# A decoder trunk's mixing stage: every projection as three products of split operands

## The chip, the core and the metric

One core of one Trainium2 chip runs the whole program in one launch. The metric is the time of that launch in device microseconds (us); lower is better. Engines are named as in the profile: PE (matrix products), PEld (its weight loads), DVE (vector), ACT (scalar), POOL and SP; here nearly all transfers are issued by SP, whose queue is worked off in order.

## What is computed

Two layers of a decoder trunk on 256 tokens of 1024 channels, in float32. Of the reference, cut to one layer:

```
h = adaLN(rms_norm(x), c)                       # 256 x 1024
p = h @ w_in + b_in                             # 1792 RWKV, 512 q, 768 k/v, 24 gate, 2048 merge columns
ya = rwkv7_mix(p[rwkv]) @ w_up_rwkv             # 8 heads of 64, a recurrence over time
yb = nsa_mix(p[q], p[kv], p[gates]) @ w_up_nsa  # compressed, selected and window attention
x += gate * ((sigmoid(p[m0]) * ya + sigmoid(p[m1]) * yb) @ w_out)
x += gate2 * moe_ffn(adaLN2(rms_norm(x), c))    # 16 experts, top 2 of one group
```

The adaLN vectors are `c @ w_ada`, 48 columns of 128 per layer.

## The kernel before, in words

Activations lie transposed: channels on the partitions, the 256 tokens along the free axis, so a projection of 128 output columns is eight matmuls (one per 128 input channels, `NK` = 8). The normalized input is `hT`, 8 x 256 float32 per partition, made by `norm_apply`: per 128 channels one DVE instruction (L261) and one ACT instruction (L262).

The mixing stage of a layer has these parts, written as steps in the string `STEPS`:
- `x` (`channels`, by `proj`, L387) projects receptance, key and value of one pair of heads; `p` (`prep`) prepares a pair, `i` (`inverse`) solves its triangular systems in blocks, `c` (`chain`) runs its recurrence over four chunks of 64 tokens. There are four pairs of heads, 0 to 3.
- `k` (`compressed`) projects the keys and values for compression and the gates, `q` (`project`) the other keys, values and queries, both by `tok` (L709). Here the tokens are the stationary operand (128 of them) and the weights stream.
- `m` (`merges`) projects the 2048 merge columns, 16 products of 128 columns; `a` (`ada_step`) reduces one piece of `w_ada` on DVE (L224, four reductions of 1024 columns and an add).
- then attention: `KZ` (L913), scores (L957), softmax, `PTs` transposes, outputs into `ybT` (L996 to L1004).

There are two ways to make a float32 product. In `proj`, `tok` and the first six `merges` (L695) operands are float32. The last ten `merges`, and the up and out projections behind the mixing stage, use `split` (L266 on ACT, L267 on DVE): an operand is written as a rounded half `hi` of type fp32r and a remainder `lo`, and `mm3` (L279) adds three products, hi-hi, lo-hi and hi-lo. For that `hT` itself is split once, after the steps.

The order on each engine isn't the text's: the framework's scheduler interleaves the steps, by priority and its own estimate of when operands are there, and each engine then works off its list in order. Weights come in blocks of 1 MB: `ringa` (3 buffers) for `in_win` and `in_cmp`, `ringd` (1 buffer) for `in_ada`. A block is loaded again into a buffer only when its last reader is through. After the mixing stage come the up projections (y), the out projections, the router, and the experts, whose 96 MB per layer stream through 18 buffers.

## Time and profile before

| | |
|---|---|
| median of 3 runs | 1205.99 us (1205.66 to 1210.89) |
| the profiled execution, its own time | 1211.18 us |
| its span, first to last instruction | 1209.4 us |
| mean granted clock of PE, as a share of full speed | 0.964 |
| busy, share of the span | PE 92%, PEld 59%, DVE 51%, ACT 29%, POOL 7% |
| moved by DMA | 328.47 MB |

Read it by stage, not by the shares of the span: mixing, up and out projections, and experts have different limits. A busy PE is not PE at its peak, since matmuls are pipelined; so the spacing of matmuls in an unbroken run is what one costs. Each float32 matmul of the program stands as two rows in the trace (224 rows for 112 matmuls of `proj` in a layer), an fp32r matmul as one.

### The profile page before, as it was taken

Reading aid. Unit: us, or ns where it says so; the run is one execution under the profiler, and the core shown is the slowest. Engines: PE = TensorE matmul, PEld = TensorE weight load, DVE = VectorE, ACT = ScalarE, POOL = GpSimd, SP = SyncE. Lnnn points to the kernel's source line nnn. Section 1 sums busy time; section 2 is a strip of 40 time slices with the busy share of each in tenths; the row PEclk is TensorE's granted clock in tenths of the full one; section 3 lists DMA queues with packets and bytes.
Section 4 is the critical chain, followed back from the end, with each engine's and each line's share of the span. In section 5 each row is a group of like instructions: output and inputs, shape, how many; then the busy total and the mean of one; then the engine's idle time right before and its main releaser. Section 6 shows DMA issues by size and latency. Waiting matters only on the chain. (4 is left out here: it accounts for less than half of the span.)

```text
span 1209.4 us, 19271 instructions
## 1 busy us (share of the span) xinstructions
PE 1112.5 (92%) x7376; PEld 710.6 (59%) x7376; DVE 617.4 (51%) x1906; ACT 349.8 (29%) x878; POOL 88.3 (7%) x176
## 2 busy tenths in 40 slices
PE   6899999989896999999789999999999789999996
PEld 3776667777895343333257776777779743333432
DVE  0497788888665222121236777777658432212222
ACT  2423322257442120201024233213565411110110
POOL 0221220100000000000022201201000000000000
PEclk9999999999998999999969899899999989999998
DMA  9753564634784999999645346254246959999991
GB/s 389 278 174 140 219 235 175 244 139 175 313 347 180 419 420 420 419 420 420 261 164 208 141 182 236 105 201 183 70 180 263 393 205 420 419 420 419 420 409 39
DMA packets 47056, 328.47 MB, mean 272 GB/s; under 512 B 5216, under 2 KB 6880, under 8 KB 7904
## 3 DMA queue, kind: packets, MB, share of 16 engines
q1 hardware_dynamic: 46512, 326.83, 67.9%
q8 instruction: 62, 1.02, 0.3%
q14 instruction: 50, 0.41, 0.1%
q10 hardware_dynamic: 432, 0.21, 0.1%
HBM read 325.98 MB, written 1.05 MB: 270 GB/s over the span
## 5 line engine op out<-in xcount | busy, mean ns | idle before, releaser
L1324 PE MATMUL ps_mm<-w,xeA 128*64 128x512 f32 x512 | 127.1, 597 | 0.0
L1335 PE MATMUL ps_mm<-w,hb 128*64 128x512 f32 (+1 forms) x576 | 124.2, 604 | 1.5 <-DMA w<-in_exp 1.2
L387 PE MATMUL ps_mm<-hT,w 128*128 128x256 f32 x448 | 115.1, 402 | 3.8 <-ACT hT L262 3.8
L224 DVE CUSTOM_DVE_ANT_0 w<-w,crow 128x1024 f32<-128x1024 f32 x80 | 98.3, 1248 | 2.7 <-POOL crow L408 2.1
L1324 PE MATMUL ps_mm<-w,xeB 128*32 128x512 f32 (+1 forms) x640 | 97.8, 595 | 0.0
L387 PEld LDWEIGHTS ps_mm<-hT,w 128*128 128x128 f32 x448 | 84.7, 198 | 19.4 <-ACT hT L262 4.3
L709 PE MATMUL ps_mm<-w,hT 128*128 128x256 f32 x320 | 86.3, 401 | 0.0
L1335 PEld LDWEIGHTS ps_mm<-w,hb 128*64 128x64 f32 (+1 forms) x576 | 36.5, 126 | 74.6 <-issue 65.3
L267 DVE TENSOR_TENSOR ys<-ps_mm,ys 128x512 fp32r<-128x512 f32 x28 | 19.2, 686 | 111.3 <-ACT ys L266 111.3
L1324 PEld LDWEIGHTS ps_mm<-w,xeA 128*64 128x64 f32 x512 | 37.1, 136 | 65.1 <-issue 61.8
L267 DVE TENSOR_TENSOR w<-w,w 128x1024 fp32r<-128x1024 f32 (+1 forms) x68 | 65.5, 970 | 16.6 <-ACT w L266 16.6
L266 ACT ACTIVATE w<-w 128x1024 fp32r<-128x1024 f32 (+1 forms) x68 | 56.2, 852 | 39.2 <-PE ps_mm L279 39.2
L1278 DVE SCALAR_TENSOR_TENSOR hb<-hb,ps_mm 128x256 f32<-128x256 f32 x28 | 11.8, 421 | 103.5 <-ACT hb L1277 103.5
L709 PEld LDWEIGHTS ps_mm<-w,hT 128*128 128x128 f32 x320 | 57.0, 193 | 9.0 <-issue 1.5
L1300 DVE SCALAR_TENSOR_TENSOR xT<-ps_rw,gfh,xT 128x256 f32<-128x256 f32 x112 | 46.6, 477 | 25.2 <-PE ps_rw L1297 25.2
L1279 DVE SCALAR_TENSOR_TENSOR hb<-ps_mm,sw,hb 128x256 f32<-128x256 f32 x28 | 12.3, 479 | 86.5 <-PE ps_mm L1324 86.5
L1324 PEld LDWEIGHTS ps_mm<-w,xeB 128*32 128x32 f32 (+1 forms) x640 | 26.0, 115 | 51.8 <-issue 48.4
L266 ACT ACTIVATE ys<-ps_mm 128x512 fp32r<-128x512 f32 x28 | 16.7, 597 | 134.0 <-PE ps_mm L1335 110.0
L1297 PEld LDWEIGHTS ps_rw<-ohT,ys 128*128 128x128 f32 x224 | 31.4, 192 | 38.7 <-ACT ys L266 19.8
L279 PE MATMUL ps_mm<-h,w 128*128 128x256 f32 x336 | 49.2, 296 | 2.5 <-DVE w L267 1.4
L279 PE MATMUL ps_mm<-m,w 128*128 128x256 f32 x384 | 51.1, 287 | 0.0
L279 PE MATMUL ps_mm<-y,w 128*128 128x256 f32 x384 | 48.3, 288 | 2.8 <-ACT w L266 2.4
(407 smaller groups left out, 1865.5 us busy)
## 6 DMA issues: line engine op xcount, KB each, us to landing
w<-in_exp SPq DMA_DIRECT2D x192, 1024.0 KB, 19.7
w<-in_ada SPq DMA_DIRECT2D x48, 1024.0 KB, 5.0
w<-in_win SPq DMA_DIRECT2D x40, 1024.0 KB, 4.9
w<-in_cmp SPq DMA_DIRECT2D x8, 1024.0 KB, 5.6
w<-in_up SPq DMA_DIRECT2D x8, 1024.0 KB, 9.0
w<-in_out SPq DMA_DIRECT2D x8, 1024.0 KB, 5.8
row<-in_row SPq DMA_DIRECT2D x2, 780.0 KB, 7.4
mis<-in_mis SPq DMA_DIRECT2D x2, 752.0 KB, 6.8
```

What stands on the lines that cost most here:

```text
L224: ve.tensor_tensor_reduce(w[:, j, :], w[:, j, :], crow, 1.0, 0.0, op0=ALU.mult, op1=ALU.add, accum_out=mod[:, o:o + 1])
L266: ac.activation(hi, x, AF.Copy)
L267: e.tensor_sub(lo, x, hi.bitcast(F32))
L279: pe.matmul(out, lhsT=w2[i][:, k, :], rhs=x2[j][:, k, :], start=(k == ks[0] and not (i or j)), stop=(k == ks[-1] and j == 1), skip_group_c ...
L387: pe.matmul(p[:, 0:T], lhsT=w[:, k, o:o + 128], rhs=hT[:, k, 0:T], start=(k == 0), stop=(k == NK - 1))
L709: pe.matmul(p[:, po_:po_ + n], lhsT=hT[:, k, tt * 128:tt * 128 + 128], rhs=w[:, k, 0:n], start=(k == 0), stop=(k == NK - 1), skip_group_ch ...
L1278: ve.scalar_tensor_tensor(h[:, o], h[:, o], 1.0, p_g[:, o], op0=ALU.add, op1=ALU.mult)
L1279: ve.scalar_tensor_tensor(h[:, o], p_u[:, o], sw, h[:, o], op0=ALU.mult, op1=ALU.mult)
L1297: pe.matmul(p[:, i * 256:i * 256 + 256], lhsT=ys[:, n, o:o + 128], rhs=ohT, start=(n == 0), stop=(n == 1), skip_group_check=True)
L1300: ve.scalar_tensor_tensor(xT[:, d, :], p[:, i * 256:i * 256 + 256], gfh[:, d:d + 1], xT[:, d, :], op0=ALU.mult, op1=ALU.add)
L1324: pe.matmul(p[o:o + n, :], lhsT=xe[:, k, x:x + n], rhs=w[:, k % 4, :], start=(k == 0), stop=(k == NK - 1), skip_group_check=True)
L1335: pe.matmul(p2[n][o:o + m, :], lhsT=hsT[:, 2 * r + g, o:o + m], rhs=w[:, g, n * 512:n * 512 + 512], start=(r + g == 0), stop=(r + g == 2), ...
```

## The change

All projections of the mixing stage go through `split` and three products. `norm_apply` writes the two halves `h2` directly: DVE computes into a scratch tile, ACT adds the shift and rounds, DVE computes the remainder. `proj` and all 16 `merges` split each weight block of 8 x 128 columns first, into one of two pairs of buffers (`wsp`, open for the whole mixing stage). `project` takes 512 columns at a time (`in_win` blocks 8 to 11 are laid out 4 x 512 for it), in four parts of 1024 columns per partition, and both token halves, so it holds two PSUM banks; it runs twice instead of four times. `compressed` streams 256 columns and the 24 gate columns together, in three parts. `ybT` moves to another pool, `y2` no longer shares memory with `h2`; `m2`, `hth` and `htl` take the memory of `h2`. Four of the nine `a` steps leave the string.

```
-STEPS = "x0 p0 x1 p1 a i0 a i1 a k c0 a b x2 p2 h0 a i2 a c1 a x3 h1 p3 i3 a a q0 z c2 c3 q1 q2 q3 m6 r"
+STEPS = "x0 p0 x1 p1 a i0 a i1 k c0 a b x2 p2 h0 i2 a c1 x3 h1 p3 i3 a q0 z c2 c3 q1 m6 r"
...
-    def norm_apply(hT, pr, G, mod, sh0):
+    def norm_apply(h2, pr, G, mod, sh0):
...
-            h = hT[:, k, 0:T]
-            ve.scalar_tensor_tensor(h, xT[:, k, :], G[:, k:k + 1], pr[:, 0:T], op0=ALU.mult, op1=ALU.mult)
-            ac.activation(h, h, AF.Identity, bias=mod[:, sh0 + k:sh0 + k + 1])
+            t = tn.tile([128, T], F32, name="nt1", tag="nt1")
+            sh = mod[:, sh0 + k:sh0 + k + 1]
+            ve.scalar_tensor_tensor(t, xT[:, k, :], G[:, k:k + 1], pr[:, 0:T], op0=ALU.mult, op1=ALU.mult)
+            ac.activation(h2[0][:, k, :], t, AF.Identity, bias=sh)
+            ve.scalar_tensor_tensor(h2[1][:, k, :], t, sh, h2[0][:, k, :].bitcast(F32), op0=ALU.add, op1=ALU.subtract)
...
+        def parts(k, n):
+
+            return [wsp.tile([128, 1024], F32R, name=f"w2{i}", tag=f"w2{i}")[:, 0:k * n].rearrange("p (k n) -> p k n", k=k)
+                    for i in range(2)]
...
-            for k in range(NK):
-                pe.matmul(p[:, 0:T], lhsT=w[:, k, o:o + 128], rhs=hT[:, k, 0:T], start=(k == 0), stop=(k == NK - 1))
+            w2 = parts(NK, 128)
+            split(*w2, w[:, :, o:o + 128])
+            mm3(p[:, 0:T], w2, h2)
...
-        def tok(tt, w, n, p, po_):
-            for k in range(NK):
-                pe.matmul(p[:, po_:po_ + n], lhsT=hT[:, k, tt * 128:tt * 128 + 128], rhs=w[:, k, 0:n],
-                          start=(k == 0), stop=(k == NK - 1), skip_group_check=True)
+        def tok(p, w2, k0, kn, n):
+
+            for tt in range(2):
+                for k in range(k0, k0 + kn):
+                    for i, j in ((0, 0), (1, 0), (0, 1)):
+                        pe.matmul(p[tt][:, 0:n], lhsT=h2[j][:, k, tt * 128:tt * 128 + 128], rhs=w2[i][:, k - k0, :],
+                                  start=(k == 0 and not (i or j)), stop=(k == NK - 1 and j == 1), skip_group_check=True)
...
-            p = ps("mm")
+            p = [ps("mm") for _ in range(2)]
+            for k0 in range(0, NK, 2):
+                w2 = parts(2, 512)
+                split(*w2, wcol(8 + 2 * j + k0 // 4)[:, k0 % 4:k0 % 4 + 2])
+                tok(p, w2, k0, 2, 512)
...
-        for k in range(NK):
-            split(h2[0][:, k, :], h2[1][:, k, :], hT[:, k, 0:T])
```

How the instructions move, at three places. First DVE in layer 0, while the last pair of heads is in its inverse (`xt` and `X`: the steps of the 8 x 8 blocks; `rs_`: a reciprocal root; `UV`, `S`, `RB`: the recurrence; `w_`: halves of a weight block). Before:

```order
L579 TENSOR_TENSOR xt<-AB,X 128x4x5
L173 TENSOR_TENSOR rs_t<-rs_t,rs_h 32x1
L580 TENSOR_TENSOR X<-X,xt 128x4x5
L175 SCALAR_TENSOR_TENSOR rs_y<-rs_t,rs_i 32x1
L579 TENSOR_TENSOR xt<-AB,X 128x4x4
L172 TENSOR_TENSOR rs_t<-rs_y 32x1
L580 TENSOR_TENSOR X<-X,xt 128x4x4
```

And now:

```order
L591 TENSOR_TENSOR xt<-AB,X 128x4x6
L172 TENSOR_TENSOR rs_t<-rs_i 32x1
L270 TENSOR_TENSOR w_2564<-w,w_2563 128x1024
L592 TENSOR_TENSOR X<-X,xt 128x4x6
L173 TENSOR_TENSOR rs_t<-rs_t,rs_h 32x1
L650 TENSOR_TENSOR S<-S,ps_rc 128x64
L591 TENSOR_TENSOR xt<-AB,X 128x4x5
```

A weight split of 1024 columns stands between two steps that wait for each other, and the recurrence of another pair is mixed in.

Second DVE at the end of layer 0's attention, where the up projections follow (`y_`: halves of `yaT` and `ybT`; `lg`: a copy for the router; L224 as `ISA`: reductions of `w_ada`). Before:

```order
L224 ISA w,mod<-w,crow 128x1024
L224 ISA mod 128x1
L267 TENSOR_TENSOR w_2994<-w,w_2993 128x1024
L226 TENSOR_TENSOR mod<-mod,vec 128x4
L267 TENSOR_TENSOR w_3024<-w,w_3023 128x1024
L243 SCALAR_TENSOR_TENSOR ng<-mod,vec 128x8
L1089 COPY lg<-ps_rc 16x128
L267 TENSOR_TENSOR y_3072<-yaT,y_3071 128x256
```

And now:

```order
L226 TENSOR_TENSOR mod<-mod,vec 128x4
L270 TENSOR_TENSOR y_3563<-ybT,y_3562 128x256
L1094 COPY lg<-ps_rc 16x128
L270 TENSOR_TENSOR y_3563<-ybT,y_3562 128x256
L224 ISA w,mod<-w,crow 128x1024
L224 ISA mod 128x1
```

The last merge splits are gone from here and the splits of `yaT` stand earlier; four reductions of `w_ada` are left, two of them ahead of the first weight split of the up projections.

Third SP at the same place, the loads of `w_ada`, of the experts and of the up and out weights. Before:

```order
L159 DMA w<-in_ada 128x2048
L1054 DMA w<-in_exp 128x2048
L159 DMA w<-in_ada 128x2048 x2
L1054 DMA w<-in_exp 128x2048 x2
L159 DMA w<-in_up 128x2048 x4
```

And now:

```order
L1058 DMA w<-in_exp 128x2048
L159 DMA w<-in_ada 128x2048 x4
L159 DMA w<-in_up 128x2048 x2
L159 DMA w<-in_ada 128x2048
L159 DMA w<-in_up 128x2048 x2
```

One load of `w_ada` now stands between the loads of the up weights.

## Rows read from the trace of the kernel before

**Rows 1.** Windows by stage: of each engine busy us (x instructions), then clock, DMA share, GB/s.

```profile
core 0: us, PE busy (x) PEld busy (x) DVE busy (x) ACT busy (x) POOL busy (x), PEclk, DMA share, GB/s
34.00:60.00 26.00, 23.70 (x103) 19.72 (x104) 11.56 (x37) 12.88 (x31) 8.58 (x22) 0.93 0.69 269
60.00:90.00 30.00, 27.60 (x167) 22.23 (x166) 27.19 (x84) 8.36 (x20) 7.51 (x11) 1.00 0.51 176
60.00:247.00 187.00, 178.75 (x1484) 133.40 (x1482) 150.11 (x506) 53.07 (x144) 32.84 (x55) 1.00 0.54 198
247.00:315.00 68.00, 61.85 (x437) 49.47 (x437) 51.61 (x180) 41.72 (x124) 0.74 (x1) 0.97 0.50 186
315.00:369.00 54.00, 53.27 (x426) 52.30 (x426) 35.20 (x66) 24.63 (x48) 0.00 (x0) 0.97 0.83 338
624.00:650.00 26.00, 22.83 (x90) 18.41 (x90) 11.85 (x25) 11.82 (x29) 7.28 (x20) 0.81 0.34 126
650.00:842.00 192.00, 185.51 (x1477) 139.16 (x1477) 147.19 (x500) 53.90 (x150) 31.01 (x57) 0.95 0.47 176
842.00:907.00 65.00, 62.41 (x461) 50.22 (x459) 38.45 (x149) 40.86 (x118) 0.00 (x0) 1.00 0.35 132
```

**Rows 2.** PE timeline, unbroken runs: start us, us, line, operands, x rows.

```profile
36.18 19.25 PE L387 MATMUL ps_mm<-hT,w 128*128 128x256 f32 x80 [2.31 <-ACT hT L262]
...
235.86 5.84 PE L695 MATMUL ps_mm<-hT,w 128*128 128x256 f32 x26
...
340.34 4.06 PE L279 MATMUL ps_mm<-m,w 128*128 128x256 f32 x32
```

**Rows 3.** Lines by form, both layers: xcount | busy us, mean ns | idle before, releaser.

```profile
L387 PE MATMUL ps_mm<-hT,w 128*128 128x256 f32 x448 | 115.1, 402 | 3.8 <-ACT hT L262 3.8
L709 PE MATMUL ps_mm<-w,hT 128*128 128x256 f32 x320 | 86.3, 401 | 0.0
L709 PE MATMUL ps_mm<-mis,hT 128*128 128x24 f32 x64 | 9.0, 285 | 0.0
L279 PEld LDWEIGHTS ps_mm<-m,w 128*128 128x128 f32 x384 | 47.5, 191 | 0.0
```

**Rows 4.** The same view, DVE and ACT.

```profile
L224 DVE CUSTOM_DVE_ANT_0 w<-w,crow 128x1024 f32<-128x1024 f32 x80 | 98.3, 1248 | 2.7 <-POOL crow L408 2.1 <-DMA w<-in_ada 0.5
L267 DVE TENSOR_TENSOR w<-w,w 128x1024 fp32r<-128x1024 f32 x36 | 44.0, 1222 | 16.6 <-ACT w L266 16.6
L266 ACT ACTIVATE w<-w 128x1024 fp32r<-128x1024 f32 x36 | 37.8, 1055 | 26.6 <-PE ps_mm L279 26.6
L261 DVE SCALAR_TENSOR_TENSOR hT<-xT,ng,rsb 128x256 f32<-128x256 f32 x16 | 6.5, 480 | 1.4 <-ACT rsb L255 1.3
L267 DVE TENSOR_TENSOR h<-hT,h 128x256 fp32r<-128x256 f32 x16 | 6.1, 444 | 0.0
```

**Rows 5.** DVE timeline at the end of layer 0's attention.

```profile
312.35 0.28 DVE L1089 COPY lg<-ps_rc 16x128 f32<-16x128 f32 x1 [7.49 <-PE ps_rc L1086]
...
315.37 2.49 DVE L267 TENSOR_TENSOR w<-w,w 128x512 fp32r<-128x512 f32 x4
```

**Rows 6.** PE timeline, from the last product of attention to the up projections, both layers.

```profile
305.41 0.59 PE L1002 MATMUL ps_rc<-PcT,VC 128*64 128x256 f32 x2
305.93 3.02 PE L279 MATMUL ps_sq<-h,w 128*128 128x256 f32 x23
...
315.36 0.39 PE L279 MATMUL ps_mm<-y,w 128*128 128x256 f32 x1 [2.44 <-ACT w L266]
...
896.75 0.59 PE L1002 MATMUL ps_rc<-PcT,VC 128*64 128x256 f32 x2
...
907.11 1.16 PE L279 MATMUL ps_mm<-y,w 128*128 128x256 f32 x5
```

**Rows 7.** The page, DMA issues: line, xcount, KB each, median us to landing.

```profile
w<-in_ada SPq DMA_DIRECT2D x48, 1024.0 KB, 5.0
```

More of the change, by code (lines that the diff above doesn't have):

```diff
@@ L683, in tile_trunk, with merges @@
         merged = iter(range(16))
[L685 removed]
+        def merges(n):
             for j in itertools.islice(merged, n):
                 w = wcol(12 + j // 2)
[L689 to L695 removed]
+                p = ps("mm")
+                w2 = parts(NK, 128)
+                split(*w2, w[:, :, 128 * (j % 2):128 * (j % 2) + 128])
+                mm3(p[:, 0:T], w2, h2)
                 ac.activation(mth[:, j, :], p[:, 0:T], AF.Tanh, scale=0.5, bias=hbm[:, j:j + 1])
@@ L900, in nt @@
             return nkb.tile([128] + shape, dt, name=name, tag=name, bufs=bufs)
-        merges(MQ, h2)
         KZ = nt([2, 2, T], "KZ")
@@ L1005, in tile_trunk @@
         dump(f"yb{l}", ybT)
-        merges(16, h2)
+        merges(16)
         while todo:
             ada_step()
-        HS.close()
         NP.close()
@@ L1061, in tile_trunk @@
             p = ps("mm")
-            w2 = [wsp.tile([128, NK, 128], F32R, name=f"w2{i}", tag=f"w2{i}") for i in range(2)]
+            w2 = [wsu.tile([128, NK, 128], F32R, name=f"w2{i}", tag=f"w2{i}") for i in range(2)]
             for i in range(2):
@@ L1066, in tile_trunk @@
                 mm3(p[:, i * 256:i * 256 + 256], w2, y2, range(4 * i, 4 * i + 4))
-            m1, m = [ms_[:, 512 * (j % 2) + 256 * i:512 * (j % 2) + 256 * i + 256] for i in range(2)]
+            ms_ = wsp.tile([128, 1024], F32, name="ms_", tag="w20")
+            m1, m = ms_[:, 0:256], ms_[:, 256:512]
             ve.scalar_tensor_tensor(m1, mth[:, 2 * j, :], 1.0, p[:, 0:256], op0=ALU.add, op1=ALU.mult)
```

76 lines of the change are left out of this document (31 added, 45 removed).

## The prediction

> **What bounds the kernel now.** I first cut the span into stages by the windows view [rows 1]. The mixing stage of a layer is its start (34 to 60, 624 to 650), the recurrence with its projections (60 to 247, 650 to 842; stage B below) and attention (247 to 315, 842 to 907). Then come 54 us of up and out projections and the experts, which the change hardly touches; they start earlier or later as a whole. So the question is how long the two mixing stages take. In stage B, PE is busy 178.75 of 187 us and 185.51 of 192, so it looks like the bound; but DVE is busy 150.1 and 147.2 there (80% and 77%), and in the densest stretch, 60 to 90, it is busy 27.19 of 30 us, 90.6%, while PE is busy 92% [rows 1]. Both engines are close to full, each works off its list in order, and each waits for the other in small pieces. In attention DVE has room, 51.6 of 68 us and 38.45 of 65 [rows 1].
>
> Next I took the price of a matmul from the spacing in unbroken runs, not from its mean duration, which counts the pipeline's latency [rows 2]. A float32 row of 256 columns: (5.84 - 0.39)/25 = 218 ns (0.39 is about one row's own length), two rows a matmul, so 436 ns. An fp32r row: (4.06 - 0.29)/31 = 122 ns, so three products cost 366 ns. At the layer's start, 80 float32 rows take 19.25 us, 239 ns each; there PE waits a little for `hT` [rows 2].
>
> **The change, part by part (per layer).**
>
> *PE, removed and added.* `proj` has 224 float32 rows, 112 matmuls [rows 3]: 112 x (436 - 366) = 7.8 us less. The first six merges are 48 matmuls: 3.4 us less. Keys, values and queries are 160 rows x 218 = 34.9 us, the gates 9.0/2 = 4.5 us [rows 3]. In their place stand 96 products of 512 columns and 48 of 280. No row shows one fp32r pass over 512 columns. It lies between one float32 row, 218 ns, and two fp32r rows, 244 ns; I take 218, since the load of the stationary side is paid once. 280 columns are 122 x 280/256 = 133 ns. That makes 20.9 + 6.4 = 27.3 us, 12.1 less. In sum PE has 23.3 us less to do per layer, 46.6 in both.
>
> The Trainium skill (TensorE: Matmul & The Clock Gate, Back-to-back issue gap) gives about 131 ns for a product of 512 columns in a sustained stream; by it the 96 products would take 12.6 us and PE would save another 8.3 us a layer. No run shows that, and the same section's 81 ns for 128 columns does not lead one to expect the 122 ns that the rows have for 256.
>
> *DVE, added.* 28 more splits of 1024 columns per layer. A split lasts 1222 ns [rows 4], but in a run they overlap: four of 512 columns take 2.49 us, so (2.49 - 0.69)/3 = 0.60 us against 0.69 alone [rows 5]; for 1024 I take 1.222 - 0.086 = 1.136. The eight times 280 columns are 2240/1024 x 1.136 and some fixed cost, 2.6 us. The norm adds eight instructions of 480 ns and loses eight of 444 [rows 4], nothing. ACT gets as many splits at 1.055 us [rows 4]; it is busy 53 of 187 us in stage B [rows 1] and hides them.
>
> *Where DVE's work lands.* By the order of the program, layer 0 has 34 splits of 1024 columns ahead of the `KZ` copy where it had 2, and 32 reductions of `w_ada` where it had 38. Six of the new splits stand in the start. Stage B so gets 26 x 1.136 + 2.6 - 6 x 1.25 = 24.7 us more. Layer 1 has 33 splits where it had 2, and the same 32 reductions: 25 x 1.136 + 2.6 = 31.0 us more.
>
> *The start.* DVE must now do 16 x 0.48 + 2 x 1.22 = 10.1 us before the first two projections can end. The other three run at 24 x 0.122 = 2.9 us each, 8.8. That makes 19 us for five projections, against 2.31 + 19.25 = 21.6 now [rows 2]. Layer 1 starts at a granted clock of 0.81 [rows 1], where sparse matmuls may keep it low; I take 0 for both.
>
> *Stage B.* PE loses 9 of its 14 projections' gain and the 12.1 us, 17.1 us, but gets about six more merges early (12 x 24 x 0.122 = 35.1 us where six float32 ones took 96 x 0.218 = 20.9): only 3 us less in all. DVE has 174.8 us in layer 0 and 178.2 in layer 1. At the 90.6% of the densest stretch [rows 1] that takes 192.9 and 196.7 us: **5.9 and 4.7 us longer**. I take that rate because splits wait for nothing but a loaded block and fill gaps; DVE at 100% would give 174.8, at the present rates of 80% and 77% 218 and 232.
>
> *Attention.* Now its tail is bare PE work. After the last product of attention at 305.41, PE does two more merges, then the splits of `y` follow, and the first up product starts at 315.36; in layer 1 the same goes from 896.75 to 907.11 [rows 6]. DVE waits 7.49 us there [rows 5]. With the merges early and `yaT` split early, about 2 us remain (copy, split, first load): 8 us less in each layer. Of the other merges that leave attention, about 3.5 in layer 0 and 2 in layer 1, 10 and 6 us of PE, I count half, 5 and 2.9 us, since attention's own chain through ACT and DVE stays. Against it in layer 0: two reductions of `w_ada` now stand ahead of the first up split on DVE. Their block has the one buffer of `ringd`, whose load can start only after the reduction before it and lands 5.0 us later [rows 7]; DVE has some 1.3 us of work meanwhile, so 3.7 us of waiting and 2.6 of reducing, 6.3 us. The last two reductions wait alike, beside PE's work on the first two up products (2 x 24 x 0.122 = 5.9 us), and cost nothing. The up loads behind them on SP are for the second half of that stage. Attention: -8 - 5 + 6.3 = **-6.6** in layer 0, -8.4 - 2.9 = **-11.3** in layer 1.
>
> *Sum.* 5.9 + 4.7 - 6.6 - 11.3 = -7.3 us against the profiled execution's own 1211.2 (span 1209.4): 1203.9. The median of the runs is 5.2 us lower, so I predict **1199 us**. A difference within 0.5%, 6 us, can't be told from none.
>
> **Rivals.**
>
> *DVE becomes the bound and holds the recurrence up (slower).* Place: stage B, where a split of 1.1 us now stands between steps of the inverse and the recurrence that wait for each other. The gains outside it are 17.9 us, so it decides where (174.8 + 178.2)/r = 379 + 17.9, at a DVE rate r of 89%. At 85% stage B takes 36.3 us more and the time is 1206 + 36.3 - 17.9 = 1224. For it: 90.6% is the best of 30 us, the mean is 80%; `project` also holds both PSUM banks of its tag, so no projection or merge can run beside it. Against it: four of the nine early `a` steps are taken out.
>
> The Trainium skill (Perfetto Trace Analysis, Identifying the Most-Contended Engine) judges PE by the share of its weight loads, not of its matmuls, and the other engines by occupancy. By it stage B of layer 0 has PE at 133.40 of 187 us, 71%, and DVE at 80% [rows 1], so the change would load the more contended engine and this rival would hold.
>
> *PE was the bound (much faster).* The new DVE work fits into gaps and the whole 46.6 us come back: 1159. For it: PE busy 96%. Against it: after the change DVE has more to do in stage B than PE's spacing asks for.
>
> *Three products cost as much as four passes.* An fp32r weight load lasts 191 ns [rows 3] and there are 624 where there were 512 rows. If loads decided, PE would get 112 x 0.194 = 21.7 us more a layer: 1249. Against it: the run at 122 ns a row, with the load of 191 ns each beside it [rows 2, 3].
>
> **How the numbers follow.** My case (rate 89 to 93%) has 0.42, of which 0.28 is faster by over 0.5% and 0.14 within. DVE the bound: 0.33, of which 0.03 within. PE the bound: 0.20. Loads: 0.05. So faster 0.48, same 0.17, slower 0.35. The range leaves out half of the case where PE gains all, and the far end of the slow ones: 1170 to 1230. My case alone spans 1187 to 1206.
>
> **What would show it.** Right: 512-column rows about 218 ns apart and 256-column ones 122; DVE at 90% from the start's end to the `KZ` copy, which comes some 5 us later than now in each layer; PE's first up product within 3 us of attention's last in layer 1, and some 8 in layer 0 with DVE waiting for `in_ada`. Wrong: the `KZ` copy 15 us or more later (first rival) or 10 us earlier (second); rows of 512 columns well off 218 ns; a granted clock in stage B below the 1.00 and 0.95 of now [rows 1].

## The result and the profile after

The changed kernel takes 1264.51 us (median of 4 runs, 1261.11 to 1273.53), the kernel before 1208.44 (4 runs, 1205.66 to 1211.6): the ratio is 1.0475, 95% interval 1.0408 to 1.0542. It is slower by 4.75%, where 1199 was forecast and 1230 was the end of the range. The profiled execution has a span of 1260.1 us against 1209.4, 50.7 more (the medians lie 56.1 apart), and a mean granted clock of 0.932 against 0.964. DVE is busy 681.0 us against 617.4, PE 1106.6 against 1112.5.

Where the 50.7 us lie is read from six marks on DVE in each kernel: the first instruction of the norm, the first `adx` of the first pair's inverse, and the first `KZ` copy, in both layers. DVE timeline of the kernel before (start us, us, engine, line, operands):

```profile
35.10 0.88 DVE L261 SCALAR_TENSOR_TENSOR hT<-xT,ng,rsb 128x256 f32<-128x256 f32 x2
...
73.61 0.41 DVE L569 TENSOR_TENSOR adx<-ad,R 128x256 f32<-128x256 f32 x1
...
247.33 0.68 DVE L913 COPY KZ<-ps_tr 64x512 f32<-64x512 f32 x1
...
626.75 0.48 DVE L261 SCALAR_TENSOR_TENSOR hT<-xT,ng,rsb 128x256 f32<-128x256 f32 x1 [1.26 <-ACT rsb L255]
...
665.70 0.43 DVE L569 TENSOR_TENSOR adx<-ad,R 128x256 f32<-128x256 f32 x1
...
843.30 0.68 DVE L913 COPY KZ<-ps_tr 64x512 f32<-64x512 f32 x1 [0.77 <-PE ps_tr L909]
```

The same marks in the changed kernel:

```profile
35.68 0.48 DVE L263 SCALAR_TENSOR_TENSOR nt<-xT,ng,rsb 128x256 f32<-128x256 f32 x1
...
87.75 0.42 DVE L581 TENSOR_TENSOR adx<-ad,R 128x256 f32<-128x256 f32 x1
...
280.96 0.68 DVE L922 COPY KZ<-ps_tr 64x512 f32<-64x512 f32 x1 [0.86 <-POOL yaT L688]
...
660.88 0.48 DVE L263 SCALAR_TENSOR_TENSOR nt<-xT,ng,rsb 128x256 f32<-128x256 f32 x1 [1.26 <-ACT rsb L255]
...
717.62 0.41 DVE L581 TENSOR_TENSOR adx<-ad,R 128x256 f32<-128x256 f32 x1
...
898.86 0.68 DVE L922 COPY KZ<-ps_tr 64x512 f32<-64x512 f32 x1 [0.86 <-POOL yaT L688]
```

The fourth mark of a layer is the first up product on PE, 315.36 and 907.11 before [rows 6], and now (PE timeline):

```profile
343.11 0.91 PE L282 MATMUL ps_mm<-y,w 128*128 128x256 f32 x2 [1.64 <-ACT w L269]
...
954.22 4.00 PE L282 MATMUL ps_mm<-y,w 128*128 128x256 f32 x18 [1.49 <-ACT w L269]
```

The differences between the marks, layer 0 / layer 1:

| stretch | before | after | more | forecast |
|---|---|---|---|---|
| norm to first `adx` (start) | 38.5 / 39.0 | 52.1 / 56.7 | 13.6 / 17.7 | 0 / 0 |
| first `adx` to `KZ` (recurrence) | 173.7 / 177.6 | 193.2 / 181.2 | 19.5 / 3.6 | 5.9 / 4.7 |
| `KZ` to first up product (attention) | 68.0 / 63.8 | 62.1 / 55.4 | -5.9 / -8.4 | -6.6 / -11.3 |
| up product to the next norm / the end | 311.4 / 302.3 | 317.8 / 305.9 | 6.4 / 3.6 | 0 / 0 |

With the 0.6 us by which the first norm begins later they add up to 50.7. The table's start reaches past the prediction's, which ended with the fifth projection. From the norm to that end it was 20.3 and 21.7 us and is now 30.4 and 34.4: 10.1 and 12.8 of the 13.6 and 17.7 lie there, the other 3.5 and 4.9 in what the prediction counted to stage B.

All stretches of one kernel come from one execution, and the kernel before alone varies between runs by up to 13 us (1204.2 to 1217.1 in the runs beside run 13), so single stretches are good to a few us only. The windows of the two starts, to be held against [rows 1]:

```profile
34.00:60.00 26.00, 15.58 (x83) 13.14 (x84) 17.79 (x37) 12.85 (x26) 8.01 (x16) 0.74 0.54 211
660.00:686.00 26.00, 17.02 (x65) 13.21 (x65) 17.09 (x32) 11.29 (x24) 5.78 (x13) 0.57 0.25 89
```

In the start PE is busy 15.58 of 26 us, where it was 23.70, at a clock of 0.74 and in layer 1 of 0.57. The recurrence alone, from the first `adx` to the `KZ` copy, layer 0 and layer 1 of the kernel before, then of the changed one:

```profile
73.61:247.33 173.72, 167.04 (x1430) 124.23 (x1430) 138.89 (x476) 48.73 (x135) 28.76 (x50) 1.00 0.55 202
665.70:843.30 177.60, 172.59 (x1419) 128.86 (x1417) 133.89 (x463) 49.72 (x139) 27.21 (x50) 0.94 0.46 173
...
87.75:280.96 193.21, 176.74 (x1589) 138.29 (x1588) 155.14 (x486) 73.22 (x162) 28.13 (x49) 0.92 0.47 174
717.62:898.86 181.24, 167.65 (x1580) 133.54 (x1581) 148.24 (x466) 71.65 (x157) 30.36 (x47) 0.96 0.47 174
```

DVE has 16.3 and 14.4 us more to do. Its share stays at 80% in layer 0 and rises from 75 to 82% in layer 1. The granted clock falls from 1.00 to 0.92 in layer 0, where 19.5 us are lost, and rises from 0.94 to 0.96 in layer 1, where 3.6 are. In layer 0 much of the low clock lies in one stretch, here in the kernel before, in the changed one, and in the version of run 5 below:

```profile
150.00:190.00 40.00, 39.69 (x355) 28.58 (x355) 32.56 (x116) 10.61 (x33) 7.90 (x9) 1.00 0.59 222
...
150.00:190.00 40.00, 34.54 (x172) 23.39 (x172) 27.31 (x94) 12.15 (x29) 4.78 (x8) 0.70 0.43 158
...
150.00:190.00 40.00, 39.15 (x308) 21.50 (x301) 30.93 (x115) 11.37 (x33) 5.48 (x9) 1.00 0.49 186
```

In the changed kernel PE is busy only 1.62 us from 156 to 160; from 160 on its clock is 0.57, then 0.50. From 180 to 190 PE is busy without a break at 0.60 while DVE is busy 55% and waits for it, 1.2 and 1.4 us at a time. Eight transposes (L534) take 3.62 us at 167, at 0.50, and 2.01 in the kernel before at the full clock. An estimate of the most that the low clock can cost, from these rows: 0.92 in the mean over 193 us, between the levels of 2.4 and 1.2 GHz, is as much as 31 us at the lower one, and at 2.01 for 3.62 PE's work in them would have taken 14 us less.

What DVE does in the start, in its timeline, with ACT's instruction between the two:

```profile
38.84 0.48 DVE L263 SCALAR_TENSOR_TENSOR nt<-xT,ng,rsb 128x256 f32<-128x256 f32 x1
39.90 0.48 DVE L265 SCALAR_TENSOR_TENSOR h<-nt,mod,h 128x256 fp32r<-128x256 f32 x1 [0.57 <-ACT h L264]
40.42 0.48 DVE L263 SCALAR_TENSOR_TENSOR nt<-xT,ng,rsb 128x256 f32<-128x256 f32 x1
```

```profile
39.36 0.51 ACT L264 ACTIVATE h<-nt,mod 128x256 fp32r<-128x256 f32 x1 [1.07 <-DVE nt L263]
```

Each 128 channels are a round trip DVE, ACT, DVE, of 40.42 - 38.84 = 1.58 us where nothing comes between (later ones take 1.8 to 2.1), because the remainder of one stands in DVE's list ahead of the next one's first instruction. Eight of them, with the two weight splits between, last from 35.68 to 51.14. PE's first product waits for the split of its weights, later ones for ACT's halves of the norm:

```profile
40.87 0.58 PE L282 MATMUL ps_mm<-h,w 128*128 128x256 f32 x1 [6.43 <-ACT w L269]
...
55.81 7.05 PE L282 MATMUL ps_mm<-h,w 128*128 128x256 f32 x48
```

In the recurrence DVE's list is served in order, and the inverse's short steps (L591, L592) stand behind long ones. Its timeline in the first inverse:

```profile
90.68 0.17 DVE L591 TENSOR_TENSOR xt<-AB,X 128x28 f32<-128x28 f32 x1
90.78 1.21 DVE L224 CUSTOM_DVE_ANT_0 w<-w,crow 128x1024 f32<-128x1024 f32 x1
...
92.00 0.17 DVE L592 TENSOR_TENSOR X<-X,xt 128x28 f32<-128x28 f32 x1
```

The long one shown is a reduction of `w_ada`, which the kernel before had, too; weight splits now stand in the list in the same way. The lines by form show the price of a weight split on DVE as assumed (1222 ns in [rows 4]), and the products of 512 columns (192, 96 a layer), whose row the prediction lacked:

```profile
L270 DVE TENSOR_TENSOR w<-w,w 128x1024 fp32r<-128x1024 f32 x92 | 112.5, 1224 | 13.4 <-ACT w L269 13.0 <-issue 0.3
L721 PE MATMUL ps_mm<-w,h 128*128 128x512 f32 x192 | 59.7, 435 | 1.3 <-DVE w L270 1.3
```

### The profile page after: what moved, and what is told of

The parts are those of the page before. It is cut to its first block, busy times and chain, and to the rows that moved or that the text cites. A ratio compares the mean times of both kernels' runs of the same rounds, so it can differ in the third digit from the quotient of the medians.

```text
span 1260.1 us, 19892 instructions
## 1 busy us (share of the span) xinstructions
PE 1106.6 (88%) x7600; PEld 715.8 (57%) x7600; DVE 681.0 (54%) x1978; ACT 407.2 (32%) x930; POOL 95.7 (8%) x176
## 5 line engine op out<-in xcount | busy, mean ns | idle before, releaser
L282 PE MATMUL ps_mm<-h,w 128*128 128x256 f32 x1824 | 276.5, 300 | 31.2 <-ACT w L269 12.2
L282 PEld LDWEIGHTS ps_mm<-h,w 128*128 128x128 f32 x1824 | 239.6, 197 | 54.4 <-ACT w L269 15.1
L270 DVE TENSOR_TENSOR w<-w,w 128x1024 fp32r<-128x1024 f32 (+2 forms) x130 | 139.3, 1075 | 18.1 <-ACT w L269 17.7
L269 ACT ACTIVATE w<-w 128x1024 fp32r<-128x1024 f32 (+2 forms) x130 | 119.9, 935 | 73.0 <-PE ps_mm L282 39.9
L224 DVE CUSTOM_DVE_ANT_0 w<-w,crow 128x1024 f32<-128x1024 f32 x80 | 98.4, 1234 | 4.2 <-POOL crow L420 2.1
L721 PE MATMUL ps_mm<-w,h 128*128 128x512 f32 (+1 forms) x288 | 77.3, 395 | 4.4 <-DVE w L270 4.3
L1303 DVE SCALAR_TENSOR_TENSOR xT<-ps_rw,gfh,xT 128x256 f32<-128x256 f32 x112 | 46.6, 477 | 23.3 <-PE ps_rw L1300 23.3
L282 PE MATMUL ps_mm<-y,w 128*128 128x256 f32 x384 | 51.6, 297 | 6.1 <-ACT w L269 4.5
L721 PEld LDWEIGHTS ps_mm<-w,h 128*128 128x128 f32 x288 | 48.1, 195 | 15.0 <-DVE w L270 5.6
L282 PEld LDWEIGHTS ps_mm<-y,w 128*128 128x128 f32 x384 | 49.5, 204 | 8.0 <-ACT w L269 6.1
L1220 PEld LDWEIGHTS ps_rw<-OH,h 128*128 128x128 f32 x256 | 36.6, 212 | 27.2 <-issue 22.7
```

What stands on the lines that cost most here:

```text
L224: ve.tensor_tensor_reduce(w[:, j, :], w[:, j, :], crow, 1.0, 0.0, op0=ALU.mult, op1=ALU.add, accum_out=mod[:, o:o + 1])
L269: ac.activation(hi, x, AF.Copy)
L270: e.tensor_sub(lo, x, hi.bitcast(F32))
L282: pe.matmul(out, lhsT=w2[i][:, k, :], rhs=x2[j][:, k, :], start=(k == ks[0] and not (i or j)), stop=(k == ks[-1] and j == 1), skip_group_c ...
L721: pe.matmul(p[tt][:, 0:n], lhsT=h2[j][:, k, tt * 128:tt * 128 + 128], rhs=w2[i][:, k - k0, :], start=(k == 0 and not (i or j)), stop=(k == ...
L1220: pe.matmul(p[:, k * 256:k * 256 + n], lhsT=h[:, tt, kk_ * 128:kk_ * 128 + 128], rhs=OH[:, tt, 0:n], start=(i == 0 and tt == 0), stop=(i = ...
```

## The experiments

All edits are to the changed kernel unless the kernel before is named. Times are medians, ratios are to the kernel before on the same chip; the kernel before has medians of 1207.7 to 1211.8 us from chip to chip, so differences in us between runs are good to some 4 us. Stretches are those of the table above, layer 0 / layer 1.

**1. The norm opened.**

```
+        ts = [rp([T], "xr" if k < 4 else "xk", XB) for k in range(NK)]
         for k in range(NK):
-            t = tn.tile([128, T], F32, name="nt1", tag="nt1")
+            ve.scalar_tensor_tensor(ts[k], ...); ac.activation(h2[0][:, k, :], ts[k], ...)
+        for k in range(NK):
+            ve.scalar_tensor_tensor(h2[1][:, k, :], ts[k], ...)
```

> Theories. T1, the start: the norm's alternation of DVE, ACT, DVE through two scratch tiles, with the first five projections behind it, costs 14 to 17 us per layer. T2, DVE's load: the remainder subtractions of the weight splits hold up the start, the first inverse and the recurrence. T3, the clock: PE with gaps runs at half clock and prolongs every chain that goes through it. Here the norm writes eight scratch tiles, so that DVE makes all eight first instructions without waiting and the remainders after them; nothing else changes. T1: about 25 us come back, 1236 to 1242 against 1264 of the change; the norm chain on DVE lasts 8 to 9 us instead of 15.4. T2 alone: 1255 to 1264, since DVE has the same work. T3: between them, the clock of the start decides.

1250.47 us, 1.0355 (1.0315 to 1.0396): 14 us back, not 25. In its DVE timeline the norm of layer 1 is now four unbroken groups, 6.4 us long:

```profile
649.77 1.67 DVE L263 SCALAR_TENSOR_TENSOR xr<-xT,ng,rsb 128x256 f32<-128x256 f32 x4 [1.26 <-ACT rsb L255]
...
654.53 1.67 DVE L267 SCALAR_TENSOR_TENSOR h<-xk,mod,h 128x256 fp32r<-128x256 f32 x4
```

The start is 48.9 / 44.5 us instead of 52.1 / 56.7, and of the 12.2 us won in layer 1 9.5 are lost again in its recurrence (190.7 against 181.2). So T1 is right about the alternation, but it is a quarter of the loss.

**2. No remainder of the weights on DVE**, in projections, merges and queries alike:

```
-            split(*w2, w[:, :, o:o + 128])
-            mm3(p[:, 0:T], w2, h2)
+            ac.activation(w2[0], w[:, :, o:o + 128], AF.Copy)
+            mm3(p[:, 0:T], (w2[0], w2[0]), h2)
```

> The weight splits of the five projections per pair, the merges and the keys, values and queries keep ACT's rounding, but DVE's remainder is left out and the rounded half stands in its place in the products; PE has exactly the instructions of the change. The compressed keys' split and the norm keep theirs. This leaves out the remainder of the weights. It takes about 54 splits of 1.1 us, some 60 us, from DVE. T2: 1205 to 1215 or less. T1: the norm is as before, so most of the loss stays: 1240 to 1250. T3: a gain only where PE's clock also comes back, to 1.00 in the mixing stages.

1201.11 us, 0.9937 (0.9910 to 0.9963). It took more from DVE than the expectation says: 76 instructions, and its busy time falls from 681.0 to 601.3, by 79.7 us. The time falls by 63.4: the whole loss is gone with as many products on PE. That is what T2 forecast, 0.8 us of time per us of DVE. But the remainder's place in the chain from block to product is gone with its time on DVE, so this run alone doesn't tell the two apart. The start is still 48.5 / 52.1 us long.

**3. The same for the 28 projections alone**, and **4. those projections in float32**, without split:

```
-            split(*w2, w[:, :, o:o + 128])
-            mm3(p[:, 0:T], w2, h2)
+            for k in range(NK):
+                pe.matmul(p[:, 0:T], lhsT=w[:, k, o:o + 128], rhs=h2[0][:, k, :].bitcast(F32), ...)
```

> Only the remainders of the 28 splits of the receptance, key and value projections are left out (the rounded half stands twice); PE has the same products as the change. About 30 us less on DVE. T2 at 63 us of time for 80 us of DVE: 24 us, 1240. Beside the float32 projections at 1248.5 it also tells PE's part: those took the same splits away and gave PE 15.6 us, so a time 8 us better than that means half of PE's time lay on the path, an equal one none. T1 alone: 1255 or more.

> The projections of receptance, key and value alone go back to float32 operands without a split, with the rounded half of the normalized input as the moving side (its remainder is left out there); merges, keys, values and queries stay as in the change. It takes 28 splits of 1024 columns from DVE and ACT, some 32 us of DVE, and gives PE 15.6 us (112 x 2 x 70 ns) back. T2: 1232 to 1240. T1: the first projections still wait for the norm's chain, though not for its remainders: 1245 to 1255. If PE were the bound, 1275 to 1280.

Without the remainders 1237.67 us, 1.0244 (1.0200 to 1.0287); in float32 1248.51, 1.0327 (1.0274 to 1.0379). Both take the same from DVE (busy 648.7 and 648.0 us); the first gains 26.8 us for 32.3 us of DVE, 0.83 each. The second gives PE 15.6 us more and is 10.8 us slower than the first: 0.7 us of time per us of PE, roughly, since the two ran on different chips and each ratio is known to 0.5%. Both engines are on the path. A projection's split takes 1.14 us of DVE and saves 0.56 us of PE, so at these prices it loses by 0.9 to 0.4.

**5. Keys, values, queries and gates in float32**, as wide as in the change:

```
-                    for i, j in ((0, 0), (1, 0), (0, 1)):
-                        pe.matmul(p[tt][:, 0:n], lhsT=h2[j][...], rhs=w2[i][:, k - k0, :], ...)
+                    pe.matmul(p[tt][:, 0:n], lhsT=h2[0][...].bitcast(F32), rhs=w2[:, k - k0, :], ...)
```

> The keys, values, queries, compressed keys and gates alone go back to float32 operands without a split, still 512 and 256 columns wide and still with both token halves in two PSUM banks, with the rounded half of the input (its remainder is left out there). It takes 24 us of DVE's splits away. T2: 1240 to 1250, by half of DVE's new work. T1: nothing in the start changes: 1258 to 1266. If the 512-column products of fp32r at 317 ns cost the time, 10 to 20 us come back in the stretch of the queries only.

1236.66 us, 1.0234 (1.0194 to 1.0275): 27.8 us for 22.7 us less DVE (658.3), more per us than any other part. The recurrences are 171.9 / 172.0 us, and their granted clock is 1.00 in both layers, where the change had 0.92 and 0.96: the low stretch of layer 0 shown above is gone, and the low clock went with DVE's load. Which of the two gave the surplus isn't separated. It isn't that this split saved PE nothing. In the changed kernel's PE timeline the products of 512 columns, 96 in a layer, stand in short runs between the recurrence's own matmuls:

```profile
197.48 0.96 PE L721 MATMUL ps_mm<-w,h 128*128 128x512 f32 x3
198.37 0.68 PE L565 MATMUL ps_rw<-TT,Xs 64*64 64x64 f32 x16
...
199.91 0.50 PE L721 MATMUL ps_mm<-w,h 128*128 128x512 f32 x1
200.34 0.68 PE L565 MATMUL ps_rw<-C,TT 64*64 64x64 f32 x16
...
218.59 2.58 PE L721 MATMUL ps_mm<-w,h 128*128 128x512 f32 x10
```

The run of ten has (2.58 - 0.50)/9 = 231 ns a product. But from a run's start to the start of what follows pass 0.89 us for three and 0.43 for one: each run costs 0.2 us beside its products. In runs of three 96 products take 32 x 0.89 = 28.5 us, not the 20.9 of the sum. The float32 rows of 256 columns that did this before stand in short runs as well, and pay the same 0.2 us:

```profile
172.60 1.13 PE L709 MATMUL ps_mm<-w,hT 128*128 128x256 f32 x4
173.66 0.68 PE L553 MATMUL ps_rw<-Tm,Al 64*64 64x64 f32 x16
```

That is 1.06 us for four, and for 128 rows 32 x 1.06 = 33.9 us where the sum had 27.9. So the saving is 5.4 us a layer where 7.0 was forecast.

**6. Opened norm and no remainders together** (the edits of 1 and 2).

> The opened norm and the weight splits without remainder together; the remainder of the weights is left out of the products. If the start's chain and DVE's load are two separate costs, their gains of 14 and 63 us add: 1187. If the subtractions were paid for mostly in the start, where the chain stands as well, 1195 to 1201. A first pair's inverse that begins 43 to 45 us after the norm (38.5 and 39.0 before the change) would show the start near what it was.

1182.57 us, 0.9779 (0.9750 to 0.9809). The two gains add, 18.5 us behind 63.4. The clock of the recurrence is 0.98 and 0.99. This is what PE's saving would be worth if the remainders cost nothing: 27 us below the kernel before. The starts, 45.7 / 43.8, are still 7 and 5 us longer than before: a split stands ahead of the first product.

**7. Only the merges split; 8. the same with the four `a` steps put back.** (7 is 1, 4 and 5 together; 8 adds this.)

```
-STEPS = "x0 p0 x1 p1 a i0 a i1 k c0 a b x2 p2 h0 i2 a c1 x3 h1 p3 i3 a q0 z c2 c3 q1 m6 r"
+STEPS = "x0 p0 x1 p1 a i0 a i1 a k c0 a b x2 p2 h0 a i2 a c1 a x3 h1 p3 i3 a a q0 z c2 c3 q1 m6 r"
```

> The opened norm, float32 operands without a split for the projections of receptance, key and value and for keys, values, queries and gates; only the 16 merges stay split and early. The rounded half of the normalized input stands for the input, so its remainder is left out in all but the merges. Sum of the single runs: 1264 - 14 - 16 - 28 = 1206. T2 says more, since with 52 splits fewer DVE is no longer close to full: 1185 to 1200, and faster than before, because the early merges keep the 6 and 10 us that attention gained. If PE is what bounds then, its 15.6 us more in the projections and the float32 queries show: 1210 or more.

> The version with the opened norm and float32 operands everywhere but in the merges (1214.2), with the four reduction steps of w_ada put back where they stood before the change; the remainder of the normalized input is left out in all but the merges. If the reductions left over in layer 0's attention cost 6.3 us there, as the prediction has it, and PE is what bounds the recurrence now: 1208, and the first up product of layer 0 about 55 us after the KZ copy instead of 60. If DVE still bounds the recurrence, the six reductions of 1.25 us that return to it cost 7 to 9 us there and the sum stays: 1214 to 1217.

1214.22 us, 1.0030 (1.0013 to 1.0048): near the kernel before, not under it. The starts are back at 38.6 / 37.9. The recurrences, 179.7 / 181.2, are 6.0 and 3.6 us longer than before, with ten or eleven early merges in place of six, and attention 6.6 us shorter in both; behind it 6.1 and 1.3 us are lost. With the steps back it is 1223.22, 1.0087 (1.0054 to 1.0121): the recurrence of layer 0 grows by 11.4 us, attention by 4.4, and 5.1 come back behind it. So the forecast's 6.3 us of stall in attention are not to be had by moving the reductions back. But the 5.1 us show what the loss behind layer 0's attention is: it comes with the leftover reductions and their loads. The first up products stand unbroken in the kernel before (first line); in the changed kernel they wait for splits (second line, one of four such waits of 0.2 to 1.2 us among the first 50); with the steps back they nearly don't (third line, run 8):

```profile
316.11 24.39 PE L279 MATMUL ps_mm<-y,w 128*128 128x256 f32 x191 [0.37 <-DVE w L267]
...
353.07 0.35 PE L282 MATMUL ps_mm<-y,w 128*128 128x256 f32 x1 [1.19 <-ACT w L269]
...
335.95 9.28 PE L284 MATMUL ps_mm<-y,w 128*128 128x256 f32 x79 [0.42 <-ACT w L271]
```

**9 to 11. The remainders on POOL**: for merges and queries (9), for merges with everything else as in 8 (10), and for merges with buffers of half the size of their own, projections split in halves on DVE (11).

```
-                split(*w2, w[:, :, 128 * (j % 2):128 * (j % 2) + 128])
+                split(*w2, w[:, :, 128 * (j % 2):128 * (j % 2) + 128], po)
...
+            for k0 in (0, 4):
+                t = wsp.tile([128, 1024], F32R, name=tag, tag=tag).rearrange("p (i k n) -> p i k n", i=2, k=4)
+                split(t[:, 0], t[:, 1], w[:, k0:k0 + 4], e)
```

The lines behind "..." are run 11's, where `tag` and `e` are "wp" and DVE for projections, "wm" and POOL for merges.

> The remainders of the 16 merges and of the keys, values and queries, 24 of the 38 weight splits of 1024 columns in a layer, go from DVE to POOL, which is busy 7 to 8% of the span; everything else is as in the change and nothing is left out. T2, if only DVE's list counts: 48 x 1.1 = 53 us off DVE, at the 63 us that 80 us of DVE gave: 40 us, 1225. If POOL is slow (its row is to show the duration) or takes DVE's time beside it, the splits come later than they did and hold the two pairs of buffers longer: 1264 or slower.

> The same with the remainders of the 16 merges on POOL (2.47 us each there, 40 us a layer), so that only merges use the two pairs of buffers; the same remainder is left out. DVE gets 18 us a layer back. If PE bounds: no more than 0 to 5 us better than the version without it. If DVE's list still delays the recurrence: 10 to 15 us better, 1193 to 1200. If POOL's 2.47 us hold the merges back, as in the run with 48 remainders on POOL (1310.6): slower, with PE waiting for POOL in attention.

> Opened norm; keys, values, queries and gates in float32 operands (the remainder of the input is left out there); projections of receptance, key and value split in two halves of four input blocks, remainder on DVE; merges the same with the remainder on POOL, with buffers of their own; the reduction steps of w_ada back. PE has 15.6 us less than in the version with float32 projections, DVE has as many splits as there. If PE bounds there: 1195 to 1203. If the split before a product is a latency that the projections' chain (ACT, DVE, PE, ACT) can't hide: 1215 to 1230, lost in the start.

1310.64 (1.0829, 1.0764 to 1.0893), 1259.15 (1.0396, 1.0366 to 1.0427) and 1263.00 us (1.0418, 1.0391 to 1.0445). POOL takes twice DVE's time for a remainder, here in run 9:

```profile
L270 POOL TENSOR_TENSOR w<-w,w 128x1024 fp32r<-128x1024 f32 x48 | 118.5, 2472 | 167.2 <-ACT w L269 158.2 <-issue 8.0 <-ACT KCZ L849 1.0
```

The Trainium skill (GPSIMD Engine Reference, Elementwise — side-by-side cycle accounting) gives POOL 1.96 times DVE's time for an addition of two float32 tensors of 2048 elements; the trace agrees, 2472 to DVE's 1224 (2.02).

The merges come late, attention takes 69.6 / 78.6, 73.5 / 73.9 and 75.3 / 77.0 us, and in 10 even the recurrences are long (188.9 / 192.3). DVE was not relieved: it has 48 remainders less to do in run 9 than in the change, some 59 us, and is busy 710.2 us instead of 681.0; in run 10 it has 32 less than in run 8 and is busy 646.8 instead of 628.0. Steps of DVE that run beside a remainder on POOL can take longer. In run 9 eight steps of the softmax take 3.70 us beside one, where eight such steps take 1.67 in the changed kernel (at 326.65):

```profile
319.28 3.70 DVE L985 TENSOR_SCALAR S<-S,sm 128x128 f32<-128x128 f32 x8
...
319.17 2.36 POOL L270 TENSOR_TENSOR w<-w,w 128x1024 fp32r<-128x1024 f32 x1 [3.24 <-ACT w L269]
```

The longest of these steps in run 9 takes 2.49 us, in the changed kernel 0.35. So the expectation's "takes DVE's time beside it" came true; how much of the loss is that and how much POOL's slowness isn't separated.

**12. PE kept busy in the norm.**

```
             ac.activation(h2[0][:, k, :], t, AF.Identity, bias=sh)
+            for _ in range(6):
+                pe.matmul(pw[:, 0:T], lhsT=h2[0][:, k, 0:128], rhs=h2[0][:, k, :], start=True, stop=True)
```

> The change itself with six products of 256 columns per 128 channels added on PE during the norm, into a PSUM tile that nobody reads: about 6 us of PE beside 15 us of waiting, to hold its clock up. T3, the clock as a cause: the first projections' 147 ns a product go back to 122 and the clock of 40 to 60 from 0.71 to 0.9 or more, 3 us per layer and perhaps as much again behind it: 1254 to 1258. If the low clock is only what waiting looks like: 1262 to 1268.

1264.63 us, 1.0425 (1.0397 to 1.0453), no gain. The clock of the start did rise, from 0.74 to 0.87:

```profile
34.00:60.00 26.00, 21.90 (x144) 19.93 (x144) 18.36 (x39) 14.78 (x29) 8.13 (x17) 0.87 0.53 201
```

Layer 0's start is 2.7 us shorter (49.4), layer 1's is not (57.1), though its clock rose as well, from 0.58 to 0.76 over the norm's first 26 us, and the whole is as slow as without. So the start's low clock isn't what lost most of the time. For the recurrence this wasn't tried.

**13. The dose, in the kernel before:** one reduction more per block of `w_ada`, nothing else.

```
             ve.tensor_tensor_reduce(w[:, j, :], w[:, j, :], crow, ..., accum_out=mod[:, o:o + 1])
+        ve.tensor_tensor_reduce(w[:, 0, :], w[:, 0, :], crow, ..., accum_out=dose)
```

> The kernel before the change, with nothing of it, and one reduction of 1024 columns more on DVE for each block of w_ada that is loaded (into a number that nobody reads; the block is held 1.25 us longer): 19 in layer 0's recurrence, 16 in layer 1's, 24 and 20 us of DVE, as many as the change adds there; PE's work is untouched. By the prediction's rate of 90.6%, DVE's (150.1 + 24)/0.906 = 192 and (147.2 + 20)/0.906 = 185 us against the 187 and 192 that it has: 5 us in layer 0 and none in layer 1, 1210 to 1216. If each us of DVE costs what the runs without remainders gave back (63 us for 80), that is 0.79 us or more: 1240 to 1260.

1252.19 us, 1.0323 (1.0294 to 1.0351): 40.4 us for 49.1 us of DVE (40 added reductions of 1227 ns). With PE's work untouched the recurrence of layer 0 is 16.8 us longer for 16 of them (20 us) by the marks; its DVE share is 152.20/190.5 = 80%, as before. But the loss isn't spread. The recurrence of layer 0 in the kernel before up to 230, and in the dosed one up to 230 and behind it:

```profile
73.61:230.00 156.39, 151.51 (x1337) 111.42 (x1338) 125.95 (x434) 43.31 (x122) 24.43 (x41) 1.00 0.53 196
...
75.50:230.00 154.50, 148.94 (x1309) 112.09 (x1308) 128.64 (x428) 41.40 (x115) 25.55 (x43) 0.99 0.50 184
230.00:266.00 36.00, 19.24 (x117) 14.26 (x115) 23.55 (x76) 5.29 (x17) 3.01 (x6) 0.66 0.53 198
```

Up to 230 the dosed kernel keeps pace, with 1309 matmuls where the other has 1337. What it loses comes behind. PE is busy 19.24 of 36 us there, at a clock of 0.66: from 241 on the last chunks of the recurrence stand alone, with no projection or merge left for PE, and twice three reductions in a row stand in their chain (PE waits 2.44 and 8.55 us for DVE). DVE isn't full there either (23.55 of 36). The price is uneven in other places, too: layer 1 loses 8.0 us for 13 reductions (16 us) at a clock of 0.95 (0.94 before), and layer 0's attention 12.4 for six, where the blocks, held longer, also come later. So the dose shows that DVE's time alone, without a split, costs about as much in the mean; it doesn't show that DVE's mean share is the cause.

**14 to 16. Less DVE in the kernel before's recurrence:** the change's string of steps alone (14), the same in layer 1 only (15), and there with three `a` steps (16).

```
-STEPS = "x0 p0 x1 p1 a i0 a i1 a k c0 a b x2 p2 h0 a i2 a c1 a x3 h1 p3 i3 a a q0 z c2 c3 q1 q2 q3 m6 r"
+STEPS = "x0 p0 x1 p1 a i0 a i1 k c0 a b x2 p2 h0 i2 a c1 x3 h1 p3 i3 a q0 z c2 c3 q1 q2 q3 m6 r"
```

> The kernel before the change with one part of it alone: the four reduction steps of w_ada leave the string (their reductions go into attention or behind it); everything else is as before, nothing is left out. Putting them back into the float32 version cost 9 us. If DVE's time in the recurrence has that price in the kernel before, too: 1196 to 1202, and the KZ copy of layer 0 some 9 us earlier. If PE bounds the kernel before: 1207 to 1215, the 6 us of stall at the up projections included.

> The kernel before with the change's string of steps in layer 1 alone (five steps of w_ada instead of nine places, for eight pieces); layer 0 as before, nothing left out. In before_no_ada layer 1's recurrence was 6.2 us shorter (672.9 to 844.3 against 665.7 to 843.3) with attention no longer (63.1 against 63.3), and layer 0 lost 7 us behind attention, where seven pieces were left over. If the two layers are independent: 1202 to 1206 against 1208 to 1212, faster than both kernels by 0.4 to 0.6%. If the 6.2 us are a chance of the schedule: no difference.

> The same with only three steps of w_ada in layer 1's string, so five pieces go to its attention, where DVE is busy 38 of 65 us. DVE has another 10 us less in layer 1's recurrence. At 0.5 to 0.8 us for each: 1195 to 1200. If the pieces that wait behind attention for their one buffer stall it, as in layer 0 of before_no_ada: 1208 to 1215.

1211.37 us, 1.0005 (0.9977 to 1.0033); 1208.73, 0.9986 (0.9959 to 1.0013); 1208.70, 1.0001 (0.9976 to 1.0026). No difference in any. In 14 the recurrences are 2.1 and 6.2 us shorter, and layer 0 loses 2.1 in attention and 7.0 behind it, as in run 7. These runs move DVE's work out of the recurrence, into attention and behind it; it isn't taken out of the program (DVE is busy 614 to 615 us in all three, 617.4 before). And of the 6.2 us in layer 1 the clock may be the cause: it is 0.94 in the profiled execution of the kernel before and 0.99 here.

**17. No split in the mixing stage at all**: 4, 5, the merges alike, and one float32 tile for the input; **18. the kernel before with all merges in float32.**

```
-            ac.activation(h2[0][:, k, :], t, AF.Identity, bias=sh)
-            ve.scalar_tensor_tensor(h2[1][:, k, :], t, sh, h2[0][:, k, :].bitcast(F32), ...)
+            ac.activation(hT[:, k, :], hT[:, k, :], AF.Identity, bias=sh)
...
-        merges(16, h2)
+        merges(16)
```

> The change's order, its 512-column queries and its early merges, but no split in the mixing stage at all: float32 operands, and the normalized input as one float32 tile, written by one DVE and one ACT instruction per 128 channels. Nothing is left out. Against the version that still splits the merges (1214.2) it takes 32 splits of 1.14 us and 16 remainders of 0.48 us from DVE, 44 us, and adds 128 x 140 ns = 18 us to PE. At the prices measured so far, 0.8 us of time per us of DVE and 0.7 per us of PE (the float32 projections against those without remainders: 11 us for 15.6): 1214 - 35 + 13 = 1192, a version faster than before. If PE bounds once DVE has room: 1214 to 1230.

> The kernel before with its last ten merges of a layer in float32 operands as well, and without the split of the input for them. Nothing is left out. DVE loses 20 splits of 1.14 and 16 remainders of 0.44 us, 30 us, most of it in attention; PE gets 80 x 2 x 70 ns = 11 us. At the same prices: 1208 - 24 + 8 = 1192 if attention follows DVE as the recurrence does; 1210 to 1218 if PE's products are what fills attention, where DVE is busy 51.6 of 68 us.

1206.64 us, 0.9985 (0.9953 to 1.0016), no difference; and 1235.14, 1.0206 (1.0161 to 1.0252). Windows of 17, recurrence and attention of layer 0:

```profile
60.00:252.00 192.00, 186.43 (x1458) 128.99 (x1456) 145.71 (x511) 53.98 (x149) 34.38 (x56) 0.99 0.50 182
252.00:313.00 61.00, 60.09 (x346) 45.95 (x346) 42.02 (x161) 31.82 (x105) 0.00 (x0) 1.00 0.58 214
```

PE is busy 97 and 99% of them, and the 1192 that the prices of 0.8 and 0.7 gave are missed by 15 us: with DVE freed, the 0.8 us per us of DVE no longer hold, and the busy share suggests that PE binds. In 18 attention grows from 68.0 / 63.8 to 77.4 / 78.0 us, 24 us in both for about 11 us more on PE: there the split of a merge is worth its DVE time. Why it costs twice PE's added work isn't settled.

Of the versions that leave nothing out, none is faster than both kernels by more than the measurement can tell.

## Why the prediction was wrong

**The step that failed first is "The start ... I take 0 for both".** The stretch to the first `adx` cost 31.3 us (13.6 + 17.7), 22.9 of them up to the end of the fifth projection. The 10.1 us of DVE were added up as if they could run back to back; but a remainder follows ACT's rounding, and in DVE's list it stands ahead of the next channels' first instruction, so the eight steps cost 1.58 us or more each and not 0.96. Opening the norm gave 14 us, and 18.5 where DVE was free (runs 1, 6). The other part is that products wait for a split that float32 products don't need: with float32 projections and the opened norm the starts are 38.6 / 37.9, as before.

**The second is "At the 90.6% of the densest stretch".** The recurrence lost 23.1 us by the marks, and 31.5 from the fifth projection on, where 10.6 were forecast for stage B. DVE's sum was near: counted from the fifth projection it has 21.1 and 19.8 us more, for 24.7 and 31.0. But its rate by the marks was 80 and 82%, near the mean of before (80 and 75%) and far from the 90.6% of the best 30 us. In layer 0 the mean of before gives the time: 155.14/0.80 = 194 us, and 193.2 were measured; at 90.6% it would be 171. In layer 1 the same rule gives 148.24/0.754 = 197 us, and it took 181.2, so the mean is no law. What holds DVE at 80% isn't settled: short steps that wait for each other behind long ones in one list are seen (the rows at 90.68), and so is a PE at half clock for which DVE waits (150 to 190). Up to 14 of the 19.5 us of layer 0 could be the clock by the estimate above. Run 12 tested it in the start only.

**PE's sum was near.** The 218 ns for 512 columns are 231 in an unbroken run, near enough; such runs are rare, and in runs of three the 20.9 us become 28.5. But the rows that they replace had the same surcharge, so of the 12.1 us of saving about 1.6 are gone. The 122 ns for 256 columns hold where the clock is full, as in run 1, (5.94 - 0.39)/47 = 118 ns; at the clock of the changed kernel's start the same 48 take 7.05 us.

```profile
51.66 5.94 PE L284 MATMUL ps_mm<-h,w 128*128 128x256 f32 x48
```

**Attention's number was near, in layer 0 by luck:** -5.9 and -8.4 us for -6.6 and -11.3. The forecast for layer 0 was -8 for the tail, -5 for merges that leave, and 6.3 for a stall. The tail, from the last product of attention to the first up product, went from 9.95 us [rows 6] to 343.11 - 339.25 = 3.86, so it gave 6.1 and held no stall of 6.3:

```profile
339.25 0.59 PE L1009 MATMUL ps_rc<-PcT,VC 128*64 128x256 f32 x2
```

What comes ahead of it is as long as before (58.3 against 58.1), so whatever the merges that left gave was lost again there. In layer 1 the tail gave 6.6 and the rest 1.8, for 8.4 and 2.9. And the work behind attention was taken as unmoved, but lost 6.4 and 3.6 us. In layer 0 the step that failed is that the last two reductions "cost nothing": with the steps put back 5.1 us came back there (run 8), and with nothing but the steps moved the kernel before lost 7.0 (run 14). For layer 1's 3.6 us no run gives a cause; in most of the other runs layer 1 loses about 1 us there or less.

**The rivals.** The first, DVE as the bound, comes nearest: it named the place and the direction, and its sign came true (the `KZ` copy of layer 0 is 33.6 us later, of which 13.6 are the start, which it did not hold). That DVE's time is the cause of most of the loss is shown by what its remainders cost (runs 2 and 3) and by the dose; that it acts as a bound, with a rate of its own, isn't. The rule on the most contended engine that was set beside it (the Trainium skill, Perfetto Trace Analysis, Identifying the Most-Contended Engine), which puts DVE's 80% above PE's 71%, pointed the right way. But DVE isn't the whole: PE's time counts too, as runs 4, 6 and 17 show, though the second rival's 46.6 us did not come. DVE's added work cost 0.8 us per us, while moving DVE's work out of the recurrence of the kernel before brought nothing in all. The sign of a granted clock below the 1.00 of before came true in layer 0 (0.92). The third rival fell: an unbroken row of 256 columns costs what the forecast said, however long its load.

Left open: how much of the loss in the recurrence is DVE's list and how much the lower clock, in the change and in the dose alike. The rows point at the clock for the difference between the layers: it fell in layer 0, and did not in layer 1, in both. A run that keeps PE's clock up in the recurrence would tell.

## What to carry to other kernels

Where two engines pass short steps to each other in order, don't price added work at the busy share of the best stretch. The mean share of the stage is the better first guess (here it was right in one layer and 15 us too long in the other), and a dose of the same work on the unchanged kernel tests it for one run; look where in the trace the dose costs its time, and at the clock there, before the price is carried over. A split that saves 0.56 us on one full engine for 1.14 on the other pays only where the second has room, as in attention here. And when a step becomes a round trip between engines, count it per trip in list order, not per instruction.
